# A planner that dates every release: banks, pages and results are handed on when the releasing instruction is done, and small jobs take ranks from a table

## The chip, the core and the metric

The kernel runs on one core of a Trainium2 chip. The core has a matrix engine (TensorE, PE in the profile, with its weight loads as PEld), VectorE (DVE), ScalarE (ACT), GpSimd (POOL), a queue engine for transfers (SyncE, SP) and 16 DMA engines. TensorE writes its sums into eight PSUM banks, which VectorE or ScalarE have to empty before a bank can be written anew; everything else lies in SBUF, here in a set of equal pages that the kernel hands out itself.

The metric is the device time of one execution in microseconds (us). Before the change it is 1189.13 us, the median of three runs (1189.07 to 1189.55).

## The reference

One inference step of a hybrid encoder layer for 1024 prompt rows and 64 rows of a running stream, model width 1024, all in float32:

- mixer: `hn = rmsnorm(h)`, `proj = hn @ w_in`, split into a gate z (512), the convolved channels x, B, C (1024), dt (8) and pooling inputs u (512). A causal convolution of four taps and SiLU; a chunked state-space scan (Mamba-2, 8 heads, state 128, blocks of 64 rows) with decays `exp(cumsum(dt * a))`; the output times `silu(z)`, with an RMS norm by groups. Beside it causal mean pooling over windows of 2, 4, 8 and 16 rows, each group times a 128x128 matrix. Both halves meet in `mix @ w_out`, and `h = h + rmsnorm(mix)`.
- FFN: `f = (silu(hn @ w_gate) * (hn @ w_up)) @ w_down` with 2816 columns, `h = h + rmsnorm(f)`.
- per-layer embedding: `e = (p @ w_ple_proj) * sigmoid(h @ w_ple_gate)`, `h = h + rmsnorm(e)`.

The outputs are h of both groups and the new states of convolution, scan and pooling.

## The kernel before

The 1088 rows lie across the free dimension in four chunks of 272 (`CH`); channels lie on the 128 partitions. A float32 product is made of three matmuls in a shorter format: weight and activation are each split into a high part (a cast, mostly on ScalarE: L495 for weights, L2706, L660) and a low part (a subtraction, mostly on VectorE, all through the helper at L448), and high·high, high·low and low·high add up in one PSUM bank (`mm3`, `run` at L528). The FFN (L2023, L2167) uses Strassen-like combinations of quarter matrices, called forms (S1 to S4, T1 to T4, A, B), which VectorE and ScalarE make.

Stages in time: input projection, convolution, scan and pooling (0 to about 260 us); the output projection with its norms, and inside it the projection of p (`w_pp`, L536, with ScalarE copies L2329 that empty its banks) to about 390; gate and up passes to about 830; the down passes to about 1060; then the gate of the embedding (`w_pg`) and the last norms. Norm statistics run as small jobs: squares are summed, split into `hi_..` and `lo_..`, and two matmuls with ones (L667, L668; for other norms L577, with L586 for the spread of the result t_..) sum over the channels. `ACT_TABLE_LOAD` appears wherever ScalarE goes from a function of one table to one of another.

No engine's order is written by hand. The Python program that emits the kernel runs a planner, the class `Layout`, while it emits. The main program emits TensorE's large products in a fixed sequence and calls `tick` (L282) for the time that each takes; everything else is a generator, a job, started by `spawn` (L255), which yields requests: `("A", 0.42)` for 0.42 us of ScalarE, `"D"`, `"E"`, `"G"` for VectorE and GpSimd, `"P"` for TensorE, `"S"` for a transfer, or a condition that must hold first. `tick` moves the planner's clock `now`, steps all jobs whose condition holds, and gives each engine the request that can start earliest, within `AHEAD` = 0.5 us of now; of those within `EPSL` = 0.2 us of each other the one of lower rank (`prio`, a number given at spawn) goes first. `until` (L338) lets the clock tick until a condition holds, such as a free bank, a page or a finished weight. What the planner does first is emitted first, so its clock sets the order on each engine, and which bank a product takes; on the chip the engines only wait for semaphores.

The conditions look at plain containers: a set of finished parts, a list of flags, a count of free buffers (`Sem`), a list of free banks (`Banks`, in order of release), free pages (`Slots`), a weight's `whole` (both parts made). A job's step that frees a bank is taken at the moment at which the planner places the instruction, which can be up to 0.5 us ahead of now, and from then on the bank counts as free.

## Time and profile before

| | before |
|---|---|
| median of three runs | 1189.13 us |
| the profiled execution: time, span | 1189.49 us, 1187.7 us |
| granted TensorE clock, mean | 0.997 |
| TensorE, weight loads | 1172.8 us, 1156.1 us |
| VectorE, ScalarE, GpSimd | 954.7, 624.9, 69.3 us |
| matmuls, VectorE, ScalarE instructions | 9429, 1806, 1303 |
| bytes moved | 178.67 MB, 150 GB/s |

The span runs from the first to the last instruction of the profiled execution; 1.8 us lie around it. Busy time of an engine is a share of that span. In the chain, each piece of time is given to what the last piece of work had to wait for. A row of a group reads: line, engine, operation, result <- operands, count, busy time, mean duration in ns, idle time just before and what ended it.

### The profile page before, as it was taken

Reading aid. Unit: us, or ns where it says so; the run is one execution under the profiler, and the core shown is the slowest. Engines: PE = TensorE matmul, PEld = TensorE weight load, DVE = VectorE, ACT = ScalarE, POOL = GpSimd, SP = SyncE. Lnnn points to the kernel's source line nnn. Section 1 sums busy time; section 2 is a strip of 40 time slices with the busy share of each in tenths; the row PEclk is TensorE's granted clock in tenths of the full one; section 3 lists DMA queues with packets and bytes.
Section 4 is the critical chain, followed back from the end, with each engine's and each line's share of the span. In section 5 each row is a group of like instructions: output and inputs, shape, how many; then the busy total and the mean of one; then the engine's idle time right before and its main releaser. Section 6 shows DMA issues by size and latency. Waiting matters only on the chain.

```text
span 1187.7 us, 23824 instructions
## 1 busy us (share of the span) xinstructions
PE 1172.8 (99%) x9429; PEld 1156.1 (97%) x9429; DVE 954.7 (80%) x1806; ACT 624.9 (53%) x1303; POOL 69.3 (6%) x67
## 2 busy tenths in 40 slices
PE   9999999999999999999999999999999999999997
PEld 7999999999999999999999999999999999999996
DVE  7796777775799899887887788778988689778955
ACT  8465557854778645343343344335664235347633
POOL 0000010310131000000000000000000000003301
PEclk9999999999999999999999999999999999999998
DMA  7113133234435336556546645567854255134512
GB/s 262 36 56 105 50 112 94 86 98 125 139 142 203 102 112 234 177 194 231 166 179 222 234 142 192 215 210 243 280 168 145 90 190 166 38 118 158 151 67 85
DMA packets 72163, 178.67 MB, mean 150 GB/s; under 512 B 8348, under 2 KB 14964, under 8 KB 72052
## 3 DMA queue, kind: packets, MB, share of 16 engines
q1 hardware_dynamic: 70932, 174.42, 43.4%
q0 software_dynamic: 976, 2.73, 0.7%
q8 instruction: 74, 1.21, 0.4%
q14 instruction: 37, 0.30, 0.1%
q10 hardware_dynamic: 144, 0.00, 0.0%
HBM read 135.67 MB, written 41.45 MB: 149 GB/s over the span
## 4 chain that ended last, share of the span: by engine, by line
PE 91%; DVE 6%; issue 1%; ACT 1%; DMA 0%; DVEq 0%; ACTq 0%
PE psall L2023 46%; PE psall L536 27%; PE psall L2167 8%; PE psall L556 3%; PE psall L1339 1%; PE psall L1310 1%; PE psall L577 1%; DVE mixf L1682 1%; PE psall L1304 1%; PE psall L1425 1%; DVE h_T L448 1%; DMA p<-af_dram 0%; PE psall L586 0%; DVE h_B L448 0%; DVE mixf L1612 0%
## 5 line engine op out<-in xcount | busy, mean ns | idle before, releaser
L536 PE MATMUL psall<-x,w_in 128*128 128x272 f32 x1440 | 192.8, 290 | 0.0
L536 PEld LDWEIGHTS psall<-x,w_in 128*128 128x128 f32 x1440 | 183.8, 188 | 4.0 <-issue 3.4
L2023 PE MATMUL psall<-h_T,w_u_S 128*128 128x272 f32 x792 | 104.2, 288 | 0.0
L2023 PE MATMUL psall<-h_T,w_g_S 128*128 128x272 f32 x792 | 101.6, 288 | 0.9 <-ACT xr L2061 0.9
L2023 PE MATMUL psall<-al_T,w_d_S 128*128 128x272 f32 x780 | 101.0, 288 | 0.3 <-ACT f L2440 0.3
L2023 PEld LDWEIGHTS psall<-h_T,w_g_S 128*128 128x128 f32 x792 | 100.1, 188 | 1.1 <-ACT xr L2061 1.1
L2023 PEld LDWEIGHTS psall<-h_T,w_u_S 128*128 128x128 f32 x792 | 101.1, 188 | 0.0
L2023 PEld LDWEIGHTS psall<-al_T,w_d_S 128*128 128x128 f32 x780 | 99.0, 188 | 0.5 <-ACT f L2440 0.5
L536 PE MATMUL psall<-mix,w_out 128*128 128x272 f32 x720 | 91.6, 288 | 0.0
L536 PEld LDWEIGHTS psall<-mix,w_out 128*128 128x128 f32 x720 | 90.7, 188 | 0.0
L2443 DVE TENSOR_TENSOR f<-f,psall 128x544 f32<-128x544 f32 (+1 forms) x96 | 60.3, 634 | 34.2 <-PE psall L2023 33.9
L536 PE MATMUL psall<-h,w_pg 128*128 128x272 f32 x576 | 74.7, 289 | 1.2 <-ACT w_pg L495 1.2
L536 PEld LDWEIGHTS psall<-h,w_pg 128*128 128x128 f32 x576 | 72.9, 188 | 1.4 <-ACT w_pg L495 1.4
L2023 PE MATMUL psall<-al_B,w_d_A 128*128 128x272 f32 x528 | 70.9, 288 | 0.3 <-DVE p L2066 0.3
L2023 PEld LDWEIGHTS psall<-al_B,w_d_A 128*128 128x128 f32 x528 | 68.0, 188 | 0.5 <-DVE p L2066 0.5
L1904 ACT CAST w_d_S<-raw_d 128x384 fp32r<-128x384 f32 (+2 forms) x55 | 27.9, 530 | 53.9 <-DVE raw_d L1939 32.6
L2061 ACT COPY p<-psall 128x544 f32<-128x544 f32 (+1 forms) x28 | 16.3, 582 | 55.0 <-PE psall L2023 55.0
L2698 POOL TENSOR_TENSOR f<-f,hr 128x544 f32<-128x544 f32 x3 | 4.1, 1365 | 702.5 <-DMA raw_pg<-in_wpg_dram 686.1
L2061 ACT COPY sq_m<-psall 128x544 f32<-128x544 f32 x24 | 14.7, 614 | 50.5 <-PE psall L2023 47.9
L2023 PE MATMUL psall<-h_B,w_g_A 128*128 128x272 f32 x288 | 38.6, 289 | 0.3 <-ACT e L2329 0.3
L2023 PE MATMUL psall<-h_B,w_u_A 128*128 128x272 f32 x288 | 38.0, 288 | 0.0
L2023 PE MATMUL psall<-al_T,w_d_A 128*128 128x272 f32 x276 | 37.5, 289 | 0.5 <-DVE f L2443 0.5
(551 smaller groups left out, 2547.1 us busy)
## 6 DMA issues: line engine op xcount, KB each, us to landing
hs_T<-hq_dram SPq DMA_DIRECT2D x36, 544.0 KB, 5.9
hs_B<-hq_dram SPq DMA_DIRECT2D x27, 544.0 KB, 4.8
raw_g<-in_wff_dram SPq DMA_DIRECT2D x22, 512.0 KB, 8.1
raw_u<-in_wff_dram SPq DMA_DIRECT2D x22, 512.0 KB, 3.8
ar_T<-af_dram SPq DMA_DIRECT2D x38, 272.0 KB, 3.2
af_dram<-sq_m SPq DMA_DIRECT2D x34, 272.0 KB, 2.9
af_dram<-p SPq DMA_DIRECT2D x33, 272.0 KB, 2.4
raw_in<-in_wmix_dram SPq DMA_DIRECT2D x15, 512.0 KB, 4.0
```

The source lines that it names most:

```text
L448: eng.tensor_tensor(lo, src, hi.bitcast(F32), ALU.subtract)
L536: pe.matmul(out, lhsT, rhs, start=i == 0, stop=i == n - 1)
L556: pe.matmul(out, w.v(wi, k), act.v(xi, k, L), start=first and n == 0, stop=not left and n == 2)
L577: pe.matmul(ps[:n, 500 + 4 * i + j:501 + 4 * i + j], acc[:, n * j:n * j + n], ones[:, 0:1], start=True, stop=True)
L1304: pe.matmul(py[:L, 256 * g:256 * g + 256], ct[:, g, t0:t0 + L], state[:, 256 * g:256 * g + 256], start=True, stop=True)
L1310: pe.matmul(pst[:, 256 * g:256 * g + 256], bk[:L, 128 * g:128 * g + 128], xw[:L, 4 * g:4 * g + 4].rearrange("p h q -> p (h q)"), start=Tru ...
L1339: pe.matmul(pyt[64 * r:64 * r + 64, P * b:P * b + L], xdt[:L, h], es[h // 4][:L, h % 4, :L], start=first, stop=True, skip_group_check=True)
L1904: ac.copy(v[:, 0], src)
L2023: pe.matmul(d[:, p - q.ps[0], :], w.v(wi, k), u.b(bf, xi, p, k), start=start and not k and not wi and not xi, stop=k == u.ks - 1 and wi == ...
L2061: ac.copy(t[:, sl], q.Z[:, pl])
L2167: pe.matmul(d, w.v(wi, k), b[:, xi, k, :], start=m in (1, 2, 5) and not k and not wi and not xi, stop=k == 1 and wi == 1, skip_group_check ...
L2443: ve.tensor_tensor(v[:, sl], v[:, sl], src[:, pl], ALU.add)
```

## The change

It touches the planner's books, its ranks and one cost; no job computes anything else.

1. Each container keeps, beside what is in it, the time at which the instruction that put it there is done (`Clk.time`). A condition that looks at it reports the latest of these times in `Clk.hit`.
2. A job whose condition comes true starts at that time, not when the planner noticed. `until` goes on only if the time is no later than now + `SOON` (0.05 us), and else lets the clock tick on. A product that takes a bank moves the clock to the bank's release. Banks are sorted by release; a bank without its free neighbour is preferred only if it is free within `SOON`.
3. The rank of a spawned job is looked up in a table `PRIO` of 75 entries by the names of the function, the form or weight and the stage (`BANDS` of planner time); where there is none, the rank in the code holds.
4. The cost of a step of dt's matmuls is 0.69 in place of 0.46 us, of the first chunk's 0.29 in place of 0.23.

`STAMP`, `SLOW`, `LATER`, `HV_Q`, `PVL`, `PQL`, `AHEAD`, `EPSL` and `PLATE` have values that leave everything as it was.

```diff
+class Clk:
+    hit, lay = 0.0, None
+    @staticmethod
+    def time():
+        return Clk.lay.done or Clk.lay.now
+    @staticmethod
+    def see(t):
+        if t > Clk.hit:
+            Clk.hit = t
+
+class TSet(set):
+    def add(self, x):
+        self.at.setdefault(x, Clk.time())
+        set.add(self, x)
+    def __contains__(self, x):
+        if set.__contains__(self, x):
+            Clk.see(self.at[x])
+            return True
+        return False
...
 class Banks:
     def take(self):
         b = self.order[0]
         if self.pairs:
-            b = next((x for x in self.order if x ^ 1 not in self.order), b)
+            far = max(Clk.time(), self.at[b]) + SOON
+            b = next((x for x in self.order if x ^ 1 not in self.order and self.at[x] <= far), b)
...
     def give(self, ap):
-        self.order.extend(self.held.pop(id(ap))[1])
+        bs = self.held.pop(id(ap))[1]
+        for b in bs:
+            self.at[b] = Clk.time()
+        self.order.extend(bs)
+        self.order.sort(key=lambda b: self.at[b])
...
+BANDS = 100, 330, 400, 475, 850, 1050
+PRIO = {
+    "SumSq.whole 6": 0.5, "a_split T1 4": 2.5, "a_stream 2": 7, "accum.step 6": 0.5, "aforms 3": 7, "aforms 4": 4,
...
 class Layout:
     def spawn(self, gen, prio=5):
...
+        key += " " + str(sum(self.now > x for x in BANDS))
+        KEYS.setdefault(key, prio)
+        prio = PRIO.get(key, prio)
...
     def tick(self, length=None):
                 if callable(req):
+                    Clk.hit = 0.0
                     if not req():
...
-                    job["t"] = max(job["t"], self.now, self.stamp if job.pop("no", False) else 0)
+                    job["t"] = max(job["t"], self.now, Clk.hit, self.stamp if job.pop("no", False) and STAMP else 0)
...
     def until(self, cond, what=""):
-        while not cond():
-            if self.fill and not self.filling and self.fill[0][0]():
+        while True:
+            Clk.hit = 0.0
+            if cond():
+                if Clk.hit <= self.now + SOON or not self.fill or self.filling:
+                    self.now = max(self.now, Clk.hit)
+                    return
+            Clk.hit = 0.0
+            if self.fill and not self.filling and self.fill[0][0]() and Clk.hit <= self.now + SOON:
                 self.filler()
                 continue
...
     def bank(name):
         until(banks.ok, "bank")
-        return jbank(name)
+        b = banks.take()
+        lay.now = max(lay.now, banks.at[b])
+        return banks.hold(psall[:, b, :], b)
...
-        yield ("P", 0.46, max(at for _, at, _ in pair))
+        yield ("P", 0.69, max(at for _, at, _ in pair))
...
-        tick(0.23)
+        tick(0.29)
```

The new kernel has the same 9429 matmuls and the same work on every engine but for ScalarE's table loads (25 in place of 19) and one transfer more on each of two queues. Lines of the same code stand some 195 to 205 lines further down. Three places where the order moved:

TensorE in the head, the statistics of the second chunk (hi_x, lo_x; xraw_.. wd is dt's product, w_in_146 to 148 three input weights). Before:

```order
L536 MATMUL psall<-x_01_98,w_in_147 128x272
L868 MATMUL psall<-xraw_0_381,wd_110 32x272 [waits DMAHW5_49]
L868 MATMUL psall<-xraw_0_381,wd_110 32x272
L868 MATMUL psall<-xraw_1_440,wd_110 32x272 [waits DMAHW6_49]
L868 MATMUL psall<-xraw_1_440,wd_110 32x272
L536 MATMUL psall<-x_01_98,w_in_147 128x272 x3
L536 MATMUL psall<-x_00_97,w_in_148 128x272 x3
L667 MATMUL psall<-hi_x_471,ones_r 128x272 [waits Activation_49]
L668 MATMUL psall<-lo_x_472,ones_r 128x272 [waits DVE_49]
```

and now:

```order
L1068 MATMUL psall<-xraw_1_417,wd_110 32x272
L732 MATMUL psall<-x_00_97,w_in_146 128x272 x4
L732 MATMUL psall<-x_01_98,w_in_146 128x272 x2
L862 MATMUL psall<-hi_x_456,ones_r 128x272 [waits Activation_49]
L863 MATMUL psall<-lo_x_457,ones_r 128x272 [waits DVE_49]
L732 MATMUL psall<-x_01_98,w_in_146 128x272 x2
L732 MATMUL psall<-x_10_99,w_in_146 128x272 x4
L732 MATMUL psall<-x_11_100,w_in_146 128x272 x4
```

The pair of statistics matmuls stood in the third weight's product and stands in the first's, 21 matmuls earlier.

TensorE at about 370 us (p_0, p_1 and w_pp: projection of p, three pairs of matmuls into one bank; t_m is a statistic of the mixer's norm). Before:

```order
L536 MATMUL psall<-p_0_3776,w_pp_3782 128x272 [waits Activation_49]
L536 MATMUL psall<-p_0_3776,w_pp_3782 128x272
L536 MATMUL psall<-p_1_3779,w_pp_3782 128x272 x2
L536 MATMUL psall<-p_0_3776,w_pp_3783 128x272 x2
L536 MATMUL psall<-p_0_3776,w_pp_3782 128x272 [waits DVE_49]
L536 MATMUL psall<-p_0_3776,w_pp_3782 128x272
L536 MATMUL psall<-p_1_3779,w_pp_3782 128x272 x2
L536 MATMUL psall<-p_0_3776,w_pp_3783 128x272 x2
L586 MATMUL psall<-cp,t_m_4468 128x68 x4
L536 MATMUL psall<-p_0_3784,w_pp_3780 128x272 [waits Activation_49]
```

and now:

```order
L781 MATMUL psall<-cp,t_m_4462 128x68 [waits DVE_49]
L781 MATMUL psall<-cp,t_m_4462 128x68 x3
L732 MATMUL psall<-p_0_3778,w_pp_3783 128x272 x2
L732 MATMUL psall<-p_1_3781,w_pp_3783 128x272 x2
L732 MATMUL psall<-p_0_3778,w_pp_3784 128x272 x2
L732 MATMUL psall<-p_0_3778,w_pp_3783 128x272 [waits Activation_49]
L732 MATMUL psall<-p_0_3778,w_pp_3783 128x272
L732 MATMUL psall<-p_1_3781,w_pp_3783 128x272 x2
L732 MATMUL psall<-p_0_3778,w_pp_3784 128x272 x2
L732 MATMUL psall<-p_0_3778,w_pp_3783 128x272 x2
```

The statistic t_m stands three projections higher, and the last projection before the next page of p no longer waits for VectorE.

ScalarE at about 1095 us (w_pg: gate weights, the last of the eight; f, h, E: pages of the residual and the embedding; L2844 is the sigmoid). Before:

```order
L2844 ACTIVATE sq_f_12270<-psall 128x544 [waits DMAHW2_49,PE_49,Pool_49]
L2706 CAST h_1_00_12825<-f_1_10457 128x544
L2689 ACTIVATE f_0_10127<-f_0_10127,cp 128x272
L2706 CAST h_1_01_12826<-f_1_10128 128x544 [waits Pool_49]
L738 ACTIVATE sg_0_12821<-E_0_12749 128x544 [waits DMAHW6_49,DVE_49]
L2838 ACTIVATE E_0_12749<-E_0_12749,cp 128x272 [waits Activation_49]
L2838 ACTIVATE E_0_12749<-E_0_12749,cp 128x272
L2844 ACTIVATE sg_0_12821<-psall 128x544 [waits DMAHW3_49,DVE_49,PE_49]
L495 CAST w_pg_12943<-raw_pg_12927 128x1024 [waits DMAHW1_49]
L2706 CAST h_1_00_12825<-f_1_9977 128x544
```

and now:

```order
L691 CAST w_pg_12837<-raw_pg_12811 128x1024 [waits DMAHW7_49]
L2892 ACTIVATE f_1_10281<-f_1_10281,cp 128x272 x2
L3047 ACT_TABLE_LOAD [waits DVE_49]
L3047 ACTIVATE hr_2_12366<-psall 128x544 [waits PE_49]
L2892 ACTIVATE f_0_10459<-f_0_10459,cp 128x272 x2
L691 CAST w_pg_12894<-raw_pg_12860 128x1024 [waits DMAHW6_49]
L2909 CAST h_1_00_12819<-f_1_10460 128x544 [waits Pool_49]
L2909 CAST h_1_00_12819<-f_1_9977 128x544 [waits DVE_49,Activation_49]
L2909 CAST h_1_01_12820<-f_1_10136 128x544 [waits Pool_49]
L3047 ACTIVATE sq_f_12604<-psall 128x544 [waits DMAHW5_49,PE_49]
```

The last cast of a gate weight stood behind the third sigmoid and stands behind the first; the eighth weight's own cast is 34 ScalarE instructions earlier.

More of the change, by code (lines that the diff above doesn't have):

```diff
@@ L110, in chunk_parts, with __init__, __len__, __ge__ @@
     return ((0, n - DEC, 0, t0), (n - DEC, DEC, 1, 0))
+class Clk:
[8 more added lines that the diff above has]
+class TSet(set):
+    def __init__(self):
+        self.at = {}
+    def add(self, x):
[6 more added lines that the diff above has]
+        return False
+    def __len__(self):
+        n = set.__len__(self)
+        if n:
+            Clk.see(max(self.at[x] for x in self))
+        return n
+    def __ge__(self, other):
+        return all(x in self for x in other)
@@ new lines, with __init__, __setitem__, __contains__ @@
+class TDict(dict):
+    def __init__(self):
+        self.at = {}
+    def __setitem__(self, k, v):
+        self.at[k] = Clk.time()
+        dict.__setitem__(self, k, v)
+    def __contains__(self, k):
+        if dict.__contains__(self, k):
+            Clk.see(self.at[k])
+            return True
+        return False
+    def get(self, k, d=None):
+        return dict.__getitem__(self, k) if k in self else d
+    def __len__(self):
+        n = dict.__len__(self)
+        if n:
+            Clk.see(max(self.at[k] for k in self))
+        return n
@@ L154, in take2 @@
     def take2(self):
-        b = min((b for b in (0, 2, 4, 6) if b in self.order and b + 1 in self.order),
-                key=lambda b: max(self.order.index(b), self.order.index(b + 1)))
+        b = self.pair()
         self.order.remove(b)
@@ L402, in bank2 @@
         b = banks.take2()
+        lay.now = max(lay.now, banks.at[b], banks.at[b + 1])
         return banks.hold(psall[:, b:b + 2, :CW], b, b + 1)
@@ L410, in bankn @@
         b = banks.take()
+        lay.now = max(lay.now, banks.at[b])
         return banks.hold(psall[:, b:b + 1, :CW], b)
@@ L470, in gen @@
             if raw is None:
-                yield lambda: wsem.ok() and slots.free() > keep()
+                yield lambda: wsem.ok() and slots.has(1 + keep())
                 wsem.take()
@@ L1773, in qforms @@
                 b[kh, p] = v[:, 2 * kh:2 * kh + 2]
-        lo = set()
+        lo = TSet()
         def form(f, src):
-            yield lambda: hsem.ok() and (spare or slots.free(True) >= 1)
+            yield lambda: hsem.ok() and (spare or slots.has(1, True))
             hsem.take()
@@ L1845, in __init__ @@
             self.keep = keep
-            self.wf, self.lo, self.r, self.room, self.forms = {}, set(), None, [], 0
+            self.wf, self.lo, self.r, self.room, self.forms = TDict(), TSet(), None, [], 0
             self.v, self.vg, self.open = False, None, 2
@@ L1853, in __init__ @@
             self.name, self.ks, self.keep, self.of = f"{'v' if blk == '11' else 'q'}{u.name}", 2, False, (g, u)
-            self.wf, self.lo, self.room, self.forms = {}, set(), [], 0
-            self.src, self.tile, self.blk, self.done, self.gone = src, tile_, blk, set(), False
+            self.wf, self.lo, self.room, self.forms = TDict(), TSet(), [], 0
+            self.src, self.tile, self.blk, self.done, self.gone = src, tile_, blk, TSet(), False
         def begin(self):
@@ L2234, in aforms @@
         tA, tD = (0.65, 0.73) if q.n == 2 else (0.42, 0.45)
-        lo = set()
+        lo = TSet()
         def form(f, t):
-            yield lambda: afs.ok() and slots.free(True) >= 1
+            yield lambda: afs.ok() and slots.has(1, True)
             afs.take()
@@ L2289, in trunk @@
     PT = {}
-    p_done = set()
+    p_done = TSet()
     pp_left = [NC * NK]
@@ L2657, in trunk @@
     H2 = [None] * NC
-    h2_k = [[] for _ in range(NC)]
+    h2_k = [TList() for _ in range(NC)]
     E = [None] * NC
```

254 lines of the change are left out of this document (170 added, 84 removed), and 18 rows, old and new, of the table PRIO.

## The prediction

> **What bounds the kernel now.** I read the page's busy line and its chain first, then the waits of TensorE, then a table by stretches of time, and last the timeline around the longest waits.
>
> ```profile
> PE 1172.8 (99%) x9429; PEld 1156.1 (97%) x9429; DVE 954.7 (80%) x1806; ACT 624.9 (53%) x1303; POOL 69.3 (6%) x67
> PE 91%; DVE 6%; issue 1%; ACT 1%; DMA 0%; DVEq 0%; ACTq 0%
> ```
>
> TensorE is busy for 99% of the span and makes 91% of the chain. The change adds and removes no matmul, so all it can touch is the time in which TensorE stands still. The view of TensorE's waits lists every one of them:
>
> ```profile
> PE psall L536 <- DVE mixf L1652: 1.6, 1, 1.6
> PE psall L966 <- DVE scr L969: 1.2, 1, 1.2
> PE psall L536 <- ACT w_pg L495: 1.2, 1, 1.2
> PE psall L586 <- DVE t_e L613: 1.1, 1, 1.1
> PE psall L2023 <- ACT xr L2061: 0.9, 1, 0.9
> PE psall L2741 <- DVE E L2737: 0.8, 1, 0.8
> PE psall L556 <- DVE h L448: 0.5, 1, 0.5
> PE psall L2023 <- DVE f L2443: 0.5, 1, 0.5
> PE psall L2167 <- DVE hv_B L448: 0.4, 1, 0.4
> PE psall L2023 <- ACT e L2329: 0.3, 1, 0.3
> PE psall L2023 <- DVE p L2066: 0.3, 1, 0.3
> PE psall L2023 <- ACT f L2440: 0.3, 1, 0.3
> ```
>
> Three of the twelve belong to the head and the tail (L966, L586, L2741: 1.2 + 1.1 + 0.8 = 3.1), where the program order stays as it was. The other nine come to 1.6 + 1.2 + 0.9 + 0.5 + 0.5 + 0.4 + 0.3 + 0.3 + 0.3 = 6.0 us. That is the ceiling of any gain: 0.5% of the span. What the change can lose has no such ceiling, since any matmul that now stands ahead of its data makes a new wait. The table by stretches says where these waits lie and how much room VectorE and ScalarE have there (busy time of each, count of instructions):
>
> ```profile
> 60.00:115.00 55.00, 55.00 (x444) 54.86 (x442) 43.80 (x84) 32.43 (x59) 0.00 (x0) 1.00 0.24 78
> 115.00:205.00 90.00, 90.00 (x730) 87.18 (x729) 71.15 (x111) 54.98 (x137) 7.04 (x13) 1.00 0.28 89
> 205.00:235.00 30.00, 30.00 (x270) 28.57 (x268) 23.62 (x53) 26.86 (x67) 7.93 (x12) 1.00 0.23 70
> 320.00:360.00 40.00, 40.00 (x322) 40.00 (x321) 38.27 (x51) 31.68 (x67) 8.99 (x6) 1.00 0.43 147
> 360.00:406.00 46.00, 43.16 (x350) 42.49 (x349) 41.00 (x54) 35.07 (x78) 4.51 (x3) 1.00 0.44 150
> 860.00:1060.00 200.00, 200.00 (x1595) 200.00 (x1594) 160.46 (x268) 87.64 (x162) 0.00 (x0) 1.00 0.42 130
> 1060.00:1112.00 52.00, 49.84 (x419) 49.01 (x418) 44.68 (x103) 38.05 (x72) 14.65 (x9) 1.00 0.50 156
> ```
>
> TensorE loses 46.00 − 43.16 = 2.84 us between 360 and 406 and 52.00 − 49.84 = 2.16 us between 1060 and 1112, five sixths of the 6.0. The row of 860 to 1060 gives the price of a place in TensorE's order: 200 us / 1595 = 125 ns for a matmul. The granted clock is 1.00 in each stretch, also where TensorE waits.
>
> **The change part by part.** The planner's bookkeeping leaves no instruction behind. What it does is another order, and per engine I compared who now stands ahead of whom, in rows of order times durations of this trace.
>
> *Stretch 355 to 406, the last quarter of the mixer.* Two of its waits:
>
> ```profile
> 371.95 1.28 DVE L1652 TENSOR_TENSOR mixf<-mixf,psall 128x1088 f32<-128x1088 f32 x1
> 373.28 1.02 PE L536 MATMUL psall<-p,w_pp 128*128 128x272 f32 x6 [1.64 <-DVE mixf L1652]
> 374.57 0.72 DVE L1612 TENSOR_TENSOR mixf<-mixf,psall 128x544 f32<-128x544 f32 x1 [1.34 <-PE psall L586]
> ...
> 405.12 0.37 ACT L2061 COPY xr<-psall 128x272 f32<-128x272 f32 x1
> 405.54 1.28 PE L2023 MATMUL psall<-h_T,w_g_S 128*128 128x272 f32 x8 [0.86 <-ACT xr L2061]
> ```
>
> A projection of p into a PSUM bank must wait until VectorE's L1652 has read that bank. It waits 1.64 us, and since the statistics matmul L586 stands right behind it, VectorE then idles 1.34 us for the result of L586. In the new order L586 stands three projections further up, and no projection near it asks for the bank that L1652 empties; they use banks that ScalarE's copies L2329 empty. So the wait of 1.6 goes, and so should VectorE's 1.34 of idle. VectorE is busy for 41.00 of 46.00 us here, so what it gains helps all that it does next: the 0.3 at L2329 (387 us) and the 0.9 at L2061 have some 1.3 us more slack by my row count. Against it, ScalarE's copies now stand up to 1.2 us of ScalarE work later than the matmuls that take their banks, and ScalarE has 46.00 − 35.07 = 10.9 us of idle in this stretch, 0.4 to 1.0 in each 10 us around 373. Bounds: 2.8 gained if all holds, 0.8 if the copies are late (1.2) and the 0.9 stays (2.8 − 1.2 − 0.9 = 0.7, say 0.8). I take +2.2, nearer the upper end, since each late copy has more idle ahead of it than it needs over 20 us. If VectorE is late again in this stretch there is no cover: the next to suffer are the first FFN matmuls at 387, which need its low parts.
>
> *Stretch 1060 to 1112, the gate of the per-layer embedding.*
>
> ```profile
> 1074.70 1.52 PE L556 MATMUL psall<-h,w_pg 128*128 128x272 f32 x10 [0.55 <-DVE h L448]
> ...
> 1095.37 0.60 ACT L2844 ACTIVATE sg<-psall 128x544 f32<-128x544 f32 x1
> 1095.87 1.03 ACT L495 CAST w_pg<-raw_pg 128x1024 fp32r<-128x1024 f32 x1
> 1096.95 0.89 PE L536 MATMUL psall<-h,w_pg 128*128 128x272 f32 x5 [1.16 <-ACT w_pg L495]
> ```
>
> TensorE waits 1.16 us for the cast of the last gate weight, which ends at 1096.90 behind a sigmoid (L2844). That cast now stands 34 ScalarE rows earlier; at 38.05 us for 72 rows these are 34 × 0.53 = 18 us of ScalarE's work, so the wait goes: +1.2. The 0.5 for h at 1074.70 shrinks by some 0.2. Against it, the sum over f of the second chunk (L577) stands 12 matmuls, 1.5 us, higher, where its data are about 0.35 us late, and one early reader of a VectorE result at about 1105 has 1.36 us more VectorE work ahead of it; VectorE has 52.00 − 44.68 = 7.3 us of idle here, but 1.2 in the 10 us before. I take −0.5 for both. Sum +0.9, between −0.3 (both in full: 1.4 − 0.35 − 1.36) and +1.4.
>
> *FFN, 406 to 1060.* The order of TensorE's 5365 matmuls there is the same one, only banks and buffers change. The 0.4 for hv_B (465) and the 0.3 for p (835) have more room by 0.4 us of VectorE's work each; the 0.3 for f (844) keeps its chain of copies. +0.6, between 0 and 0.7.
>
> *Head, 20 to 47 us.* The statistics of the second and third chunk (L667, L668) move up on TensorE:
>
> ```profile
> 28.63 0.43 DVE L923 TENSOR_TENSOR acc_x<-acc_x,sqx 128x272 f32<-128x272 f32 x1
> 29.35 0.40 ACT L660 CAST hi_x<-acc_x 128x272 fp32r<-128x272 f32 x1
> 29.79 0.44 DVE L448 TENSOR_TENSOR lo_x<-acc_x,hi_x 128x272 fp32r<-128x272 f32 x1 [0.31 <-ACT hi_x L660]
> 31.97 0.29 PE L667 MATMUL psall<-hi_x,ones_r 128*128 128x272 f32 x1
> ```
>
> TensorE's row 187 becomes row 166: 21 matmuls, 2.9 us with the slower ones among them (what now is row 166 starts at 29.0), so it arrives at about 29.0. The cast of hi and the subtraction of lo come one row earlier on their engines, some 0.4 us: lo is done at 29.79 + 0.44 − 0.4 = 29.8. New wait: about 0.6, and the third chunk, which moves by 24 matmuls, gets 0.1 to 0.5 by the same count. I take −0.7; the bounds are 0 (VectorE uses the idle it has) and −1.5.
>
> *Scan and pooling, 60 to 300 us.* TensorE never waits here before (55.00, 90.00 and 30.00 of as much). Scan matmuls stand 20 to 50 rows later than their inputs, pooling matmuls up to 66 rows earlier, and ScalarE alternates more often between Exp and Silu: 25 table loads in place of 19, four of the new ones between 60 and 135 us, two between 189 and 245. Their price has its rows:
>
> ```profile
> L1253 ACT ACT_TABLE_LOAD x4 | 5.1, 1283 | 0.1
> ...
> 203.46 0.41 ACT L1505 ACTIVATE sq_g<-xs 128x272 f32<-128x272 f32 x1
> 203.90 1.28 ACT L1253 ACT_TABLE_LOAD   x1
> 205.19 1.15 ACT L1253 ACTIVATE e<-e 128x512 f32<-128x512 f32 x2
> ```
>
> A load takes 1.28 us, and here starts 0.03 us after the instruction ahead of it: 6 × 1.28 = 7.7 us of ScalarE. Between 60 and 115 us ScalarE has 55.00 − 32.43 = 22.6 us of idle, from 115 to 205 it has 35.0, which cover them. If that cover were gone each load would cost its 1.28. Between 205 and 235 it has only 3.1, but four loads of the new order lie there where five do now. The tightest place is the first pooling group: its matmuls come at 198.4 in place of 206.6 us, and counted in rows ScalarE can have the cast that they read done by about 196.5, if it starts on time at 189.7. The Trainium skill ("ScalarE: Activation LUTs", section "What ACT_TABLE_LOAD costs") gives 1283 ns for the load and a drain of about 1380 ns beside it, 2.66 us for a switch, and asks to batch by set, which speaks against this change. The load agrees with the row of 1283 ns; of the drain the 0.03 us ahead of the load and the 0.01 behind it show nothing. By the page the six would be an estimated 16.0 us of ScalarE, and by the row 7.7.
>
> *All other moves* (statistics of the gated norm at 260 to 290, of the mixer's norms at 300 to 355, the forms at 480 to 510): each needs 0.4 to 1.2 us more work done by its time, with 1 to 6 us of idle before it. Together with the scan I take −0.5, between 0 and −2.
>
> **Sum.** +2.2 + 0.9 + 0.6 − 0.7 − 0.5 = 2.5 us gained; all low ends together −3.0 (0.8 − 0.3 + 0 − 1.5 − 2), all high ends +4.9 (2.8 + 1.4 + 0.7). The profiled execution of 1189.49 us (span 1187.7) becomes 1187.0. It is 0.36 above the median of the runs; from the median, 1189.13 − 2.5 = 1186.6 us, a gain of 0.21%.
>
> **The rivals.**
>
> *No change.* VectorE stays full from 320 to 406 (38.27 of 40, then 41.00 of 46). A wait removed at 373 only lets TensorE arrive 1.6 us earlier at data that VectorE makes at its own pace, so the same time is lost at 387 and 405. For it: the 5 us of idle, most of which is waiting for TensorE. Against it: that idle, at 374.57, goes away with the wait. Of the sum remain 0.9 + 0.6 + 0.5 (what the stretch keeps) − 1.2 = 0.8: 1188.3 us. A change of the planner's books whose orders differ without effect gives the same.
>
> *Slower: ScalarE falls behind in the scan.* If ScalarE is late at 189.7 by more than the 1.9 us between 196.5 and 198.4, TensorE waits at the first pooling group, and from there at each copy out of PSUM, as ScalarE (26.86 of 30.00) cannot catch up before 235. Priced at four of the six loads, 5.1 us, against the 2.5: 1191.7 us. For it: TensorE's new order leans on ScalarE 8.2 us earlier there. Against it: ScalarE's idle of 35.0 us just before. With the drain of the Trainium skill ("ScalarE: Activation LUTs", the section named above) on two more loads, 2 × 1.38 = 2.8 us, it would be an estimated 1194.5; the rows show no drain.
>
> *All waits go.* All nine vanish and nothing new appears: 1189.13 − 6.0 = 1183.1 us. Against it: the new early arrivals in the head and the unchanged chains at 844 and 1068.
>
> **How the numbers follow.** Forecast 0.47, no change 0.28, slower 0.14, all waits gone 0.11. The forecast's own range is 1184.9 to 1187.9. The terms' bounds (+4.9 and −3.0 from 1189.13) give 1184.2 to 1192.1. To hold 8 in 10, I cut the slow end, where only the slower rival lies, to 1190.4, and reach to 1183.4, towards the case of all waits. A measurement of this kernel tells about 0.2%, 2.4 us, from no change: faster means under 1186.75. To it go two thirds of the forecast (0.32, its lower part is within), the case of all waits, 0.11, and 0.05 of the rest: 0.48. Slower by over 0.2% is the slower rival but for its mild part, and a little of the second: 0.14. Within: 0.38.
>
> **What would show it.** In the changed kernel's waits of TensorE the rows for L1652 and the last w_pg cast must be missing, the row for L2061 at or under 0.3; the row 360 to 406 must show TensorE at 45.2 or more. A wait of L667/L668 on lo_x of 0.4 to 1.1 in the head should be new. ScalarE's busy time must be up by 7.7, with no wait on ScalarE between 60 and 300. Wrong would be a TensorE wait on ph or bk near 198 to 235, on copies L2329 over 1.2 near 365 to 375, or on VectorE's low parts at 387 to 406.

## The result: slower, 0.42%

The changed kernel takes 1194.51 us, the median of six runs (1193.19 to 1196.80), beside 1189.53 for the kernel before in as many (1189.07 to 1191.83): a ratio of 1.0042, 95% interval 1.0027 to 1.0056. The forecast was 1186.6 with a range up to 1190.4. The profiled execution took 1193.26 us, its span is 1191.5 in place of 1187.7; it ran at a granted clock of 0.997 as the profile before did, while three of the six runs had 0.995 and took 1195.3 to 1196.8, so the profiles differ by 3.8 us and the medians by 5.0.

The page's busy line and its chain:

```profile
PE 1174.7 (99%) x9429; PEld 1156.7 (97%) x9429; DVE 951.7 (80%) x1806; ACT 632.9 (53%) x1309; POOL 71.7 (6%) x68
PE 91%; DVE 5%; ACT 2%; DMA 1%; issue 1%; SPq 0%; DVEq 0%
```

ScalarE has 8.0 us more, six table loads and little else. New in the chain is a share of 1% for DMA, 11.5 us in which the end of the kernel hung on two transfers: 6.9 on that of the parameter row cp in the head, and 4.6 on that of a gate weight, raw_pg. The view of TensorE's waits, of the changed kernel:

```profile
PE psall L772 <- DVE sq_f L959: 1.8, 1, 1.8
PE psall L772 <- DVE el L959: 1.3, 1, 1.3
PE psall L1166 <- DVE scr L1169: 1.2, 1, 1.2
PE psall L781 <- DVE t_f L842: 1.1, 1, 1.1
PE psall L781 <- DVE t_e L808: 1.1, 1, 1.1
PE psall L772 <- DVE acc_g L1707: 1.0, 1, 1.0
PE psall L2944 <- DVE E L2940: 0.8, 1, 0.8
PE psall L1412 <- DVE dta L1404: 0.7, 1, 0.7
PE psall L732 <- DVE w_in L644: 0.6, 1, 0.6
PE psall L2226 <- DVE f L2646: 0.5, 1, 0.5
PE psall L781 <- DVE t_f L823: 0.5, 1, 0.5
PE psall L781 <- DVE t_x L823: 0.4, 1, 0.4
PE psall L732 <- DVE w_pg L644: 0.2, 1, 0.2
```

Of the nine waits that could be won, eight are gone; only the 0.5 for f at 1069 us stays. In their place stand new ones, none of them between 230 and 1060 us: w_in and t_x in the head, dta and acc_g in the scan, t_f, sq_f and el in the gate stage. Two rows of the table by stretches show both sides (TensorE, weight loads, VectorE, ScalarE, GpSimd):

```profile
360.00:406.00 46.00, 46.00 (x379) 45.83 (x378) 43.85 (x57) 37.45 (x84) 4.51 (x3) 1.00 0.43 149
1060.00:1112.00 52.00, 46.57 (x386) 45.28 (x384) 46.87 (x95) 37.25 (x71) 15.63 (x8) 1.00 0.48 150
```

Between 360 and 406 TensorE is never idle (2.84 us before). Between 1060 and 1112 it is idle for 5.43 us (2.16 before).

Both programs issue the same 9173 matmuls (the profile counts 9429, since 256 of them leave two rows each). So one can set the start of the n-th matmul of the program in one trace against the start of the n-th in the other. The difference is the lag behind the kernel before, and its growth over a stage is what the stage lost or won. This table has it for the changed kernel and for the experiments below (us, minus is won; from the start of the first matmul to the 300th, and so on; the last column is the lag at matmul 9100, near the end):

| kernel | head, to 300 | dt chain, to 600 | scan and pooling, to 2700 | mixer end and FFN, to 8200 | gate, to 9100 | sum |
|---|---|---|---|---|---|---|
| the change | +2.53 | +1.32 | +1.33 | −5.30 | +3.78 | +3.66 |
| 1 pool_b late | +0.41 | +1.34 | +1.29 | −5.51 | +3.77 | +1.30 |
| 2 dating alone | +2.68 | +0.02 | +0.06 | +2.23 | +2.41 | +7.40 |
| 3 ranks alone | +0.04 | +1.15 | +0.96 | −1.23 | +2.74 | +3.66 |
| 4 middle only | −0.28 | 0.00 | +0.18 | −5.38 | +0.20 | −5.28 |
| 5 dt rank back | +0.61 | +0.03 | +1.71 | −3.67 | +3.64 | +2.32 |
| 6 gate by the old books | +0.51 | +1.34 | +2.91 | −4.44 | +0.26 | +0.58 |
| 7 pg_3 not on GpSimd | +0.14 | +1.33 | +1.28 | −4.07 | +1.44 | +0.12 |
| 8 dating, form ranks | +0.38 | +0.03 | +0.07 | −4.51 | +2.35 | −1.68 |
| 9 decay rank back | +0.33 | +1.29 | +1.72 | −5.11 | +3.65 | +1.88 |
| 10 dated to 1050, form ranks | +0.62 | +0.02 | −0.06 | −4.47 | +0.08 | −3.81 |
| 11 dated to 1050, ranks | +0.54 | +0.02 | +0.05 | −4.19 | +0.21 | −3.37 |
| 12 middle, pg_3 not on GpSimd | −0.24 | 0.00 | +0.04 | −5.40 | +1.66 | −3.94 |
| 13 pool rank back | +0.89 | +1.33 | +1.88 | −4.01 | +3.61 | +3.70 |
| 14 evac rank back | +0.70 | +1.34 | +0.90 | −3.73 | +4.18 | +3.39 |

The cut at matmul 600 falls among matmuls that moved: the dt chain's own matmuls now lie ahead of it and are missing behind it, so some 0.4 of the 1.32 in that column is no idle time. The two columns together, 2.65 us, are what the changed kernel lost between the head and matmul 2700.

Some cells hold up to 2 us that no change of order made. In 6, seven matmuls at 220 to 223 us take double their time, with the granted clock at 0.50 from 220 to 223 (1.6 us). In 3, 5, 13 and 14 a run of 14 to 17 matmuls of the gate stage starts 0.23 us apart in place of 0.125, with the clock at 0.50 in the two microseconds from 1104, in 3 from 1112 (1.4 to 1.8 us). In 5, 7, 13 and 14 TensorE waits 1.16 us more for f at 846 us, although its order there is that of experiment 1. So a single cell is read with the waits beside it.

**Where the four losses come from.** In the head, VectorE's row of the changed kernel, beside the same instruction of the kernel before:

```profile
12.54 0.16 DVE L1232 TENSOR_TENSOR cp<-cp 128x4 f32<-128x4 f32 x1 [2.18 <-DMA cp<-in_par_dram]
```

```profile
18.09 0.15 DVE L1032 TENSOR_TENSOR cp<-cp 128x4 f32<-128x4 f32 x1
```

It is the product of two parameter rows, pool_b and pool_scale, needed much later. Its transfer is issued at 5.6 us and lands at 12.5. The new planner puts it at place 12 of VectorE's order in place of 26, and VectorE with all that stands behind it, the low parts of the input weights above all, waits for 2.18 us. In the dt chain and the scan (VectorE, TensorE and ScalarE of the changed kernel):

```profile
78.95 0.23 DVE L1404 SCALAR_TENSOR_TENSOR dta<-dt,ea 128x72 f32<-128x72 f32 x1
79.23 0.89 PE L1412 MATMUL psall<-dta,cp 128*128 128x72 f32 x6 [0.70 <-DVE dta L1404]
...
211.71 1.28 ACT L1453 ACT_TABLE_LOAD   x1
214.18 1.28 ACT L1683 ACT_TABLE_LOAD   x1
215.93 0.44 DVE L1690 TENSOR_TENSOR xs<-xs,z 128x272 f32<-128x272 f32 x1 [3.61 <-ACT z L1683]
221.12 0.65 PE L772 MATMUL psall<-cp,acc_g 128*68 128x1 f32 x8 [1.02 <-DVE acc_g L1707]
```

The dt chain, 177 TensorE rows earlier (row 527 in place of 704), comes to a dta that is not ready. At 211.71 ScalarE makes an Exp pair with a table load ahead and one behind it, 3.8 us, and only then the gate z; VectorE stands idle for 3.61 us, and the sum of squares acc_g that it makes next comes 1.02 us late; that the one makes the other is read from these rows, and experiments 9, 13 and 14 leave it open. In the gate stage (GpSimd, the transfer queue, ScalarE, VectorE):

```profile
1076.42 5.01 POOL L644 TENSOR_TENSOR w_pg<-raw_pg,w_pg 128x1024 fp32r<-128x1024 f32 x1 [6.28 <-DVE h L644]
1076.98 1.21 DVE L644 TENSOR_TENSOR w_pg<-raw_pg,w_pg 128x1024 fp32r<-128x1024 f32 x1
1081.46 0.81 SPq L617 DMA_DIRECT2D raw_pg<-in_wpg_dram  x2
1086.49 1.05 ACT L691 CAST w_pg<-raw_pg 128x1024 fp32r<-128x1024 f32 x1 [7.66 <-DMA raw_pg<-in_wpg_dram]
1087.58 1.23 DVE L644 TENSOR_TENSOR w_pg<-raw_pg,w_pg 128x1024 fp32r<-128x1024 f32 x1 [3.27 <-ACT w_pg L691]
```

This is one chain. GpSimd's low part of the gate weight pg_3 takes 5.01 us and holds until 1081.43 the page that the transfer of pg_6 needs. pg_5's transfer stands behind pg_6's in the queue's order, so both start at 1081.46 (the x2 of the third row). Its own page had come free at 1078.20, when VectorE's low part of pg_2 was done (the second row); pg_4 and pg_7 had taken the pages that came free before. ScalarE's cast that waits 7.66 us is pg_5's, with the sigmoid and all other work behind it; VectorE's low part of the same weight waits 3.27 us more with the norms behind it. From there VectorE is full (23.4 of the 24 us from 1088 to 1112), and the statistics sq_f and el come 1.8 and 1.3 us late. In the kernel before the transfers went in the order pg_0 to pg_7, and pg_5's started 11.0 us earlier. Of these, 7.7 are the later page and 3.3 the place behind pg_6. Its row in the transfer queue of that kernel:

```profile
1070.47 0.33 SPq L421 DMA_DIRECT2D raw_pg<-in_wpg_dram  x1
```

The changed kernel issues them in the order 1, 0, 4, 7, 2, 3, 6, 5: pg_4 and pg_7 went ahead, and pg_5 went last, though TensorE needs it before pg_7 (from matmul 8474 of the program, pg_7 from 8526). The cast of pg_5 kept its place among ScalarE's work (row 1206 in place of 1200, and six table loads stand ahead of it); only its transfer was moved.

### The profile page after: what moved, and what is told of

Same layout as the page of the kernel before. It is cut to its first block, busy times and chain, and to the rows that moved or that the text cites. A ratio compares the mean times of both kernels' runs of the same rounds, so it can differ in the third digit from the quotient of the medians.

```text
span 1191.5 us, 23829 instructions
## 1 busy us (share of the span) xinstructions
PE 1174.7 (99%) x9429; PEld 1156.7 (97%) x9429; DVE 951.7 (80%) x1806; ACT 632.9 (53%) x1309; POOL 71.7 (6%) x68
## 4 chain that ended last, share of the span: by engine, by line
PE 91%; DVE 5%; ACT 2%; DMA 1%; issue 1%; SPq 0%; DVEq 0%
PE psall L2226 48%; PE psall L732 27%; PE psall L2370 9%; PE psall L751 2%; PE psall L1510 1%; PE psall L1539 1%; PE psall L772 1%; PE psall L1504 1%; DMA cp<-in_par_dram 1%; PE psall L1625 0%; ACT x L1093 0%; DMA raw_pg<-in_wpg_dram 0%; PE psall L2711 0%; ACT sqx L1116 0%; SPq L617 0%
## 5 line engine op out<-in xcount | busy, mean ns | idle before, releaser
L2387 DVE TENSOR_TENSOR sq_m<-sq_m,psall 128x272 f32<-128x272 f32 x92 | 39.5, 434 | 22.6 <-PE psall L2370 22.4
L2107 ACT CAST w_g_S<-raw_g 128x512 fp32r<-128x512 f32 x34 | 20.5, 619 | 56.9 <-PE psall L2226 33.7
L644 POOL TENSOR_TENSOR w_pg<-raw_pg,w_pg 128x1024 fp32r<-128x1024 f32 x2 | 7.6, 3799 | 686.5 <-ACT w_pg L691 680.2
L2264 ACT COPY sq_m<-psall 128x544 f32<-128x544 f32 (+1 forms) x44 | 26.1, 592 | 42.2 <-PE psall L2226 42.2
L2107 ACT CAST w_u_S<-raw_u 128x512 fp32r<-128x512 f32 x34 | 20.9, 621 | 45.4 <-DVE raw_u L2142 41.0
L2107 ACT CAST w_d_A<-raw_d 128x384 fp32r<-128x384 f32 (+2 forms) x43 | 22.1, 525 | 36.4 <-PE psall L2226 32.1
```

The source lines that it names most:

```text
L2107: ac.copy(v[:, 0], src)
L2264: ac.copy(t[:, sl], q.Z[:, pl])
L2387: ve.tensor_tensor(t, t, d, ALU.add)
```

## The experiments

The theory after the result (A): each loss is an in-order engine that stands behind one instruction whose transfer or cast is late, place by place, and the places add up. Against it (B): TensorE's new order itself comes ahead of its data, as the prediction had it for the head; and (C): ScalarE's table loads cost what they last.

Beside the experiments 1 to 4 the kernel before took 1190.15 us, beside 5 to 8 1189.30, beside 9 to 12 1189.71, and beside 13 and 14 1189.33. So runs of different groups are compared by their ratios to it.

### 1: the pool_b product late

```diff
     def gt_job():
-        yield ("D", 0.16, 10)
+        yield ("D", 0.16, 16)
```

> The changed kernel with one number altered: the small VectorE job that multiplies pool_b by pool_scale asks to run 14.7 us after the start in place of 9.2; in VectorE's order that one instruction moves from place 12 to 30 and nothing else moves. Theory A (each loss is an in-order engine standing behind one instruction whose transfer or cast is late): VectorE's wait of 2.18 us for the parameter transfer at 12.5 us goes, TensorE's lag behind the kernel before at its matmul 300 falls from 2.55 us to 0.3 to 0.9, the time falls by 1.5 to 2.5 us to about 1192 to 1193, and the runs, which spread over 3.6 us, come within 1 us, since the landing of that transfer varied. Theory B (the head is lost by TensorE's own order, statistics ahead of their data): the lag stays above 2, the time at 1194.5.

Measured: 1192.43 us (ratio to before 1.0020, interval 1.0011 to 1.0029). The instruction runs without a wait, the lag at matmul 300 is 0.41 us, and all other columns of the table stay where they were:

```profile
19.96 0.16 DVE L1232 TENSOR_TENSOR cp<-cp 128x4 f32<-128x4 f32 x1
```

One instruction of 0.16 us at the wrong place made 2.1 us of the loss. B falls for the head: the statistics stand as high as in the changed kernel and are waited for by no row of the waits. The part on the scatter missed: these runs spread over 2.8 us.

### 2 and 3: dating alone, ranks alone

```diff
-        prio = PRIO.get(key, prio)
+        if key[-1] in '':
+            prio = PRIO.get(key, prio)
```

The first is 2: the rank in the code always holds. The second is 3: `Clk.on()` is never true, so no release is dated, banks are not sorted, and `tick` and `until` work as in the kernel before.

```diff
+DATED = ()
...
     def see(t):
-        if t > Clk.hit:
+        if t > Clk.hit and Clk.on():
...
-        yield ("P", 0.69, max(at for _, at, _ in pair))
+        yield ("P", 0.46, max(at for _, at, _ in pair))
...
-        tick(0.29)
+        tick(0.23)
```

> The changed kernel with an empty table of ranks: dated releases and the new dt cost alone. 19 table loads, the dt chain back behind, the pool_b instruction still at place 12. If the dating gives what was won between 360 and 1060 us (5.3 us against the kernel before): TensorE's lag falls by 3 us or more there. If the ranks give it: by less than 1.5. In the head theory A expects VectorE's wait of about 2 us and a lag of 2 to 3; at 79 and 221 us no wait. Time 1187.5 to 1190.5 if the dating wins the middle, 1190.5 to 1194 if the ranks do.

> The planner of the kernel before (no dated releases, old dt cost) with the new table of ranks. 25 table loads, the dt chain early, the pool_b instruction at place 25 as before. Theory A: no wait for the parameter transfer in the head, lag there under 1 us; waits near 79 us (dta) and 221 us (group norm behind the table loads), 0.7 to 1.2 each. If the ranks win the middle: the lag falls by 3 us or more between 360 and 1060; if the dating does: by less than 1.5. Time 1186 to 1189 if the ranks win the middle, 1190 to 1193 if not.

Dating alone: 1197.40 us (1.0061, 1.0049 to 1.0074), outside both ranges named. It wins 3.8 us between matmul 2700 and 3500, from a lag of 2.76 to a lead of 1.02, and then it loses 6.7 us in one place:

```profile
467.93 0.65 ACT L1926 CAST hv_B<-mixf 128x544 fp32r<-128x544 f32 x1 [3.89 <-DVE hv_T L645]
468.63 0.59 PE L2371 MATMUL psall<-hv_B,w_vu_S 128*128 128x272 f32 x1 [4.49 <-ACT hv_B L1926]
```

```profile
468.60:473.60 5.00, 4.80 (x19) 4.50 (x20) 3.50 (x6) 2.38 (x4) 0.00 (x0) 0.50 1.01 350
```

The cast of the form hv_B stands behind a subtraction that VectorE does late, and TensorE waits 4.65 us from start to start. The row of the stretch right behind it has the granted clock at 0.50: 18 matmuls start 0.23 us apart in place of 0.125, which makes the other 2 us. Ranks alone: 1193.46 us (1.0030, 1.0020 to 1.0040), 0.5 above the range named. It has no wait for the parameter transfer, a lag of 0.04 us at matmul 300, both waits of dta (0.6) and acc_g (1.0), and only 1.23 us won in the middle. So the win in the middle is the dating's, and it can be had only where ranks keep the forms on time; the waits for dta and acc_g come with the ranks, that for the parameter transfer with the dating.

### 4: both, in the middle only

```diff
+DATED = ((330, 1050),)
...
+        if key[-1] in '2345':
             prio = PRIO.get(key, prio)
...
-        yield ("P", 0.69, max(at for _, at, _ in pair))
+        yield ("P", 0.46, max(at for _, at, _ in pair))
```

Outside these planner times the old `tick` and `until` are in force.

> Dated releases and ranks only while the planner's clock is between 330 and 1050 us, the planner, ranks and dt cost of the kernel before outside. The order is that of the kernel before up to 320 us. If gains and losses belong to their stages and add up: no lag up to 360, a lead of 4 to 5 us by 1000 us, and in the gate stage the waits of the kernel before (2.2 us) or somewhat more: 1184 to 1186.5. If the gain of the middle in the changed kernel was only the return of time lost before it (engines that had run ahead while TensorE was late): a lead under 2 us and 1187.5 or more.

Measured: 1185.90 us, ratio 0.9965 (0.9953 to 0.9978): faster than before by 0.35%, clear of noise. The lead at matmul 8200 is 5.48 us, so the win is no mere return of time lost earlier. The waits of TensorE and two rows of the stretches:

```profile
PE psall L1187 <- DVE scr L1190: 1.2, 1, 1.2
PE psall L802 <- DVE t_e L829: 1.1, 1, 1.1
PE psall L2965 <- DVE E L2961: 0.8, 1, 0.8
PE psall L753 <- ACT sq_f L3068: 0.4, 1, 0.4
PE psall L2247 <- DVE f L2667: 0.4, 1, 0.4
PE psall L793 <- DVE sq_f L980: 0.3, 1, 0.3
PE psall L772 <- DVE h L665: 0.3, 1, 0.3
PE psall L753 <- DVE w_pg L665: 0.3, 1, 0.3
```

```profile
360.00:406.00 46.00, 46.00 (x380) 46.00 (x379) 40.54 (x57) 35.27 (x80) 4.03 (x3) 1.00 0.52 173
1060.00:1112.00 52.00, 50.17 (x411) 48.95 (x410) 48.20 (x98) 40.10 (x76) 16.32 (x10) 1.00 0.48 147
```

Beside head and tail 1.7 us of waits are left, all in the gate stage. VectorE, which I had called full between 360 and 406, does its part in 40.54 of 46 us without a wait of TensorE.

### 5: the dt chain's rank back

```diff
+for x in ('dt_chain 0',):
+    del PRIO[x]
```

This and the runs 6, 7, 9, 13 and 14 stand on experiment 1.

> The first experiment's kernel (pool_b instruction at place 30) and, beside it, no rank for the dt chain in the table, so that the chain keeps the rank 4 of the kernel before in place of 0. 13 TensorE rows move, table loads fall from 25 to 21. Theory A (places add up): TensorE's wait for dta at 77 us (0.87 us start to start) goes, the lag behind the kernel before at its matmul 900 falls from 1.57 to 0.4 to 0.9, the time by 0.7 to 1.2 us against the first experiment. The wait of 1.16 us at 219 us stays if it comes from the Exp and SiLU order of the scan itself, and goes if it comes from the loads near 100 us. Rival (ScalarE's table loads cost what they last): 4 x 1.28 = 5.1 us less, the time near 1187.5.

Measured: 1192.04 us (1.0021, 1.0010 to 1.0031), by the ratios no less than experiment 1 (1.0020). The two waits of its scan, of 0.7 and 1.0 in experiment 1:

```profile
PE psall L774 <- DVE acc_g L1709: 1.0, 1, 1.0
PE psall L1414 <- DVE dta L1406: 0.2, 1, 0.2
```

The wait for dta shrinks and the other stays. The column of the dt chain falls from 1.34 to 0.03, but the lag at matmul 900 only from 1.57 to 0.98, above the 0.9 that A allowed, and the time not by the 0.7 to 1.2 us named: the place is A's, the size is not. C is missed by far: four table loads fewer, 5.1 us of ScalarE, are not seen in the time.

### 6 and 7: the gate stage

```diff
+DATED = ((0, 1050),)
...
+        if key[-1] in '012345':
             prio = PRIO.get(key, prio)
```

```diff
-LOW_G = ('pg_3', 'pg_4')
+LOW_G = ('pg_4',)
```

> The first experiment's kernel with the planner and ranks of the kernel before from planner time 1050 us on. Nothing moves before 1050 us. If the dated releases and the ranks make the loss of the gate stage (from a lead of 2.5 us at 1054 to a lag of 1.3 at 1169 in the first experiment, 3.8 us), it falls under 1 us and the time by about 3, to 1189 to 1190. If the loss comes from the place of pages and transfers that the FFN leaves behind, it stays over 2.5.

> The first experiment's kernel, but the low part of gate weight pg_3 is made by VectorE and not by GpSimd, where it took 5.0 us and ended at 1081.4, with the transfers of the last two gate weights queued behind it on the transfer queue, ScalarE's cast 7.7 us and VectorE 3.3 us behind them. Theory A (one late transfer blocks ScalarE and then VectorE): the transfers start 3 us earlier or more, ScalarE's wait of 7.7 us falls under 4, TensorE's waits between 1085 and 1112 (1.3 + 0.4 + 1.9 + 1.4 = 5.0 us start to start) fall to 2 to 3, the time by 2 to 3. Rival (VectorE has simply too much work in this order): VectorE gets 1.2 us more, the waits stay or grow, the time stays within 1 us or rises.

With the old books from 1050 us on (6): 1189.79 us (1.0002, 0.9993 to 1.0012), and the gate stage loses 0.26 us. With the low part of pg_3 on VectorE (7): 1190.31 us (1.0007, 0.9998 to 1.0016), by the ratios 1.5 us less than experiment 1. The transfer queue and ScalarE of 7:

```profile
1077.07 0.33 SPq L617 DMA_DIRECT2D raw_pg<-in_wpg_dram  x1
1080.99 0.38 SPq L617 DMA_DIRECT2D raw_pg<-in_wpg_dram  x1
```

```profile
1081.51 1.05 ACT L691 CAST w_pg<-raw_pg 128x1024 fp32r<-128x1024 f32 x1 [3.87 <-DMA raw_pg<-in_wpg_dram]
```

In 7 pg_5's transfer is the first of the two and starts when its own page is free, no longer behind GpSimd. That is 4.4 us earlier than in the changed kernel, of which 1.2 are only that this run is ahead by then. ScalarE's wait halves, VectorE's wait of 3.27 us is gone, and the stage loses 1.44 in place of 3.77 us, although VectorE has 1.2 us more to do. In 6 that transfer starts nearly as late as in the changed kernel (1079.75, ahead of pg_6's), and yet its cast waits little:

```profile
1083.31 1.05 ACT L712 CAST w_pg<-raw_pg 128x1024 fp32r<-128x1024 f32 x1 [0.41 <-DMA raw_pg<-in_wpg_dram]
```

There ScalarE has a sigmoid, its table load and other work ahead of the cast. So a late transfer alone costs little; it costs where the cast that reads it stands ahead of work that could have been done. Both outcomes are A's.

### 8, 10 and 11: what of the middle is needed

```diff
+        if key[-1] in '3':
             prio = PRIO.get(key, prio)
```

This is 8, with pool_b late; 10 adds `DATED = ((0, 1050),)`, and 11 has that and `'2345'`.

> The changed kernel with ranks only in the stage from 400 to 475 us (the forms of the FFN's first passes), none elsewhere, and pool_b late as in the first experiment. In the kernel with dating alone TensorE waited 4.65 us at 468.6 us for a form (hv_B) whose cast stood behind a late VectorE subtraction. If the table's ranks for these forms are what mends that: the wait is under 1 us, the lead between matmuls 2700 and 8200 grows to 4 to 5.5 us as in the kernel with the middle alone, no lag before 360 over 0.6, and the time is 1187 to 1189. If ranks of other stages mend it: a wait of 3 us or more stays, 1191 or more.

> Dated releases up to planner time 1050 us, ranks only for the stage from 400 to 475, pool_b late, new dt cost, the old planner for the gate stage. If the stages add up: the eighth experiment's 1188.2 less the 2.0 to 2.4 us of its gate stage, 1185.8 to 1186.4, a lead of 4 us at matmul 8200 that stays to the end. If the gate needs the state that its own planner leaves: a loss of 1 us or more there, 1187 or more.

> As the tenth experiment, but with the table's ranks for all stages from 330 to 1050 us. Against the tenth it shows what the ranks outside 400 to 475 are worth: if they help in 475 to 860 (waits of 0.5 and 0.3 us at 830 and 840 us go), 0.5 to 0.9 less, 1185.0 to 1185.7; if not, the same within 0.4.

Experiment 8: 1188.23 us (0.9992, 0.9982 to 1.0001). The 20 ranks for 400 to 475 us (of 83 in the program's table) alone take away the wait of 4.65 us for hv_B; there is no wait at all between 60 and 360 us, and the gate loses 2.35. Experiment 10: 1185.95 (0.9970, 0.9960 to 0.9981), the gate loses 0.08, as added up. Experiment 11: 1185.81 (0.9970, 0.9959 to 0.9982), the same as 10: the ranks for 330 to 400 and for 475 to 1050 us are worth nothing that can be measured.

### 9, 13 and 14: the wait for acc_g

```diff
+for x in ('decay 1',):
+    del PRIO[x]
```

13 takes out `pool_post 1` (2.5) and 14 `proj_evac 1` (3) in the same way.

> The first experiment's kernel without the rank of the scan's decay job in the stage from 100 to 330 us (rank 4 of the kernel before in place of 3). 25 table loads as before; what moves is the place of an Exp pair and its two loads on ScalarE, which now stand behind the squares of the first group norm and not ahead of them. If TensorE's wait of 1.16 us for the group norm at 219 us comes from these squares standing behind the pair (3.8 us of ScalarE): it goes and the time falls by 1.0 to 1.4 against the first experiment, to about 1191.2. If it comes from the number of loads: it stays, 1192.4.

> The first experiment's kernel without the rank 2.5 of the pooling job in the stage from 100 to 330 us (3 as in the kernel before). If the wait of 1.16 us at 219 us comes from the last pooling group having moved ahead, with its bank copies and casts on ScalarE ahead of the squares of the group norm: it falls under 0.4, the lag behind the kernel before at matmul 1900 from 3.0 to 1.6 to 2.2. If the pooling group has no part in it: the wait stays within 0.3.

> The first experiment's kernel without the rank 3 for emptying projection banks in the stage from 100 to 330 us (0 as in the kernel before: ahead of everything). If the wait at 219 us comes from VectorE emptying a bank late, so that the gate z comes late to ScalarE and with it the table loads: it falls under 0.4. If not: it stays within 0.3, and VectorE's idle time of 3.6 us for z at 216 stays too.

All three missed. 9 (1192.09 us, 1.0022, 1.0013 to 1.0031) has a smaller wait for acc_g and a new one for pl, the low part of the first pooling input; 13 (1193.28 us in one run) has a smaller one and a new one for t_g; 14 (1192.94 in one run) keeps 0.7. From start to start the wait for acc_g costs 0.82, 0.54 and 0.86 us in them, and 1.16 in experiment 1. The waits of 9 and 13 between 60 and 360 us:

```profile
PE psall L1627 <- DVE pl L646: 0.8, 1, 0.8
PE psall L1414 <- DVE dta L1406: 0.7, 1, 0.7
PE psall L774 <- DVE acc_g L1709: 0.7, 1, 0.7
```

```profile
PE psall L783 <- DVE t_g L844: 0.8, 1, 0.8
PE psall L1414 <- DVE dta L1406: 0.7, 1, 0.7
PE psall L774 <- DVE acc_g L1709: 0.4, 1, 0.4
```

In each VectorE stands idle for ScalarE somewhere between 210 and 216 us: 2.26 and 3.59 us in 9, 2.44 in 13, 4.37 in 14, where the idle time for z falls to 1.14. What is shown is that the stage loses its 0.9 to 1.9 us only with the ranks up to 330 us in force (1, 3, 5, 7, 9, 13 and 14 have them; 2, 4, 8, 10, 11 and 12 do not, and lose at most 0.18). Which rank does it stays open: with one taken back the column has 1.72, 1.88 and 0.90 in place of 1.29.

### 12: the middle only, pg_3 on VectorE

> The fourth experiment's kernel (dating and ranks from 330 to 1050 us, else the planner of the kernel before) with the low part of gate weight pg_3 made by VectorE and not by GpSimd. If GpSimd's slow subtraction is what delays the last transfers in the old gate order too: the waits left there (2.2 us) fall by 0.5 to 1 and the time to 1185.0 to 1185.5. If VectorE is the limit there: 0 to 1 us more than the fourth, 1186 to 1187.

Measured: 1186.63 us (0.9979, 0.9970 to 0.9988), by the ratios 1.7 us more than experiment 4. Its gate stage loses 1.66 in place of 0.20, and TensorE has 2.5 us of waits there for h, in four pieces, in place of 0.3. The same edit that helps the new gate order hurts the old one. In experiment 4 the cast of pg_6 does not wait for its transfer, so GpSimd's subtraction seems to hold nobody up there, and VectorE's 1.2 us do; that these make the waits for h is argued, not shown.

## Why the prediction was wrong, point by point

- **What bounds the kernel.** Right: TensorE's waits were all there was to win, and what it could lose had no ceiling. The listed waits were the right ones, eight of nine went.
- **355 to 406 and FFN, +2.2 and +0.6.** The mechanism was right and the size too small: 5.30 us in the changed kernel and 5.38 in experiment 4, which has nothing else. The idle time of a wait is not its whole price: from the start of the matmul ahead to that of the waiting one, less the 0.13 us of a matmul, the six waits cost 1.80, 0.51, 1.02, 0.53, 0.46 and 0.42, 4.7 us, in place of the 3.8 that the view of waits gives. Some 0.6 us of the 5.3 these waits do not account for. And the lateness of ScalarE's copies for which I took off 0.6 did not come.
- **Head, −0.7.** The size was wrong by 1.8 and the cause was another. I priced statistics matmuls that come early; their wait on lo_x did not come, and with the pool_b product later the whole head loses 0.41. The price that decided, 2.18 us for one instruction of 0.16, was not in the sum: I had counted work, and this instruction has none; what counted was the transfer that it waits for.
- **Scan and pooling, within −0.5.** It lost 2.65: 1.32 by matmul 600, with the dt chain, which moved up by 177 rows and which the prediction does not name, and 1.33 behind it, with the wait for acc_g. The rival of a late ScalarE was near the truth in its mechanism (an Exp pair between two table loads, VectorE idle behind it) and wrong in its price: 1.3 us, not 5.1, and the wait came at 221 us, not at the 198 named. Of the loads, the row was the right price; the Trainium skill ("ScalarE: Activation LUTs", section "What ACT_TABLE_LOAD costs") has a drain beside each, and ScalarE's busy time rose by 8.0 us, six times 1.28 and 0.3, with next to no idle time beside the loads. The estimated 1194.5 that the prediction gives with that drain lies beside the measured 1194.51 by luck: no drain is seen, and the loss was made in four places, three of which that rival does not have.
- **Gate, +0.9.** This is the step that failed most: it lost 3.78. The wait for pg_7's cast went as said ("That cast now stands 34 ScalarE rows earlier", "so the wait goes"). But the term followed only the cast and what it overtakes on ScalarE. Its transfer moved up too, past pg_5's in the transfer queue, and another weight paid: pg_5's transfer went from 1070.47 to 1081.46, with a page that came free later and behind a transfer that GpSimd held up, and a cast that had kept its place made all that stands behind it wait. The prediction spoke of VectorE's 7.3 us of idle as cover; 3.27 of them were spent on that one wait.
- **Rivals.** "Slower" had 0.14 and one mechanism in one stage. The likeliest way to slower, a small instruction moved ahead of its own transfer, was not among them. "No change" was refuted for the middle: VectorE follows when TensorE comes earlier. None of the signs that the prediction named as wrong was seen: no wait on ph or bk, none over 1.2 on the copies, none on low parts at 387 to 406. They watched other tiles than those that came late.

## What to carry to other kernels

An instruction that an order moves up has to be followed back to what it waits for, its transfer above all, and that transfer to whom it overtakes in its own queue, before one counts what the instruction passes: on an in-order engine or queue one wait becomes the wait of everything behind it, and the shorter the instruction the easier it is missed. A planner that dates releases must date transfers too; two of the four places where it lost, 5.9 of the 9.0 us, are places where it had no such date (a fixed 9.2 us for a parameter row, a page held by a slow GpSimd subtraction). The rest came with the ranks. And a change to a planner is worth taking apart by stages: here the same change won 5.3 us in one and lost 9.0 in others, and kept to the one it makes the kernel 0.35% faster than before.

## What the runs showed of the hardware beyond that

VectorE and GpSimd can hold each other up. GpSimd's subtraction ran from 1076.42 to 1081.43. VectorE's instructions up to 1079.19 took their usual time beside it, but then an operation on 68x4 elements, 0.17 us elsewhere, took 1.70:

```profile
1079.76 1.70 DVE L828 TENSOR_SCALAR t_f<-t_f 68x4 int32<-68x4 int32 x1
```

It ended at 1081.46, with GpSimd's, and GpSimd's own instruction took 5.01 us. In the kernel before it took 2.40, from 1069.35, and there VectorE's subtraction beside it took 2.25 us, 0.71 elsewhere:

```profile
1070.08 2.25 DVE L448 TENSOR_TENSOR h<-f,h 128x544 fp32r<-128x544 f32 x1
```

The Trainium skill ("SBUF — State Buffer", section "Terms") says that the two share a pair of ports which one holds for a whole instruction while the other blocks. The trace agrees for these two instructions; why others of VectorE passed meanwhile is not shown.

TensorE's matmuls can run at half their rate for some microseconds after a wait. In experiment 2 the granted clock was 0.50 for the 5 us behind the wait of 4.49 us, and 18 matmuls started 0.23 us apart in place of 0.125. Runs 3, 5, 13 and 14 have such a stretch after waits of 1.3 to 1.8 us, and the changed kernel has none after waits of 1.8 and 1.3, so the length of the wait alone does not decide it here.

The time of one and the same program goes with the granted clock in part: the six runs of the changed kernel took 1193.2 to 1193.8 us at 0.996 to 0.997 and 1195.3 to 1196.8 at 0.995. In experiment 1, though, the run at the lowest clock, 0.993, took 1192.43, the median. Two thousandths of 1190 us are 2.4 us, as much as the effects in question, so here only lags and waits within a trace, or many runs, tell them apart.
